# Sums of weights in DRAM that start in attention's first unit, five accumulations ahead of the differences of values

## The chip, the core and the metric

The kernel runs on one core of one Trainium2 chip. Its time is device microseconds of one execution, from the first to the last instruction with what lies around them. A core has five engines with a queue of instructions each: PE (TensorE, matmul), DVE (VectorE), ACT (ScalarE), POOL (GpSimd) and SP (SyncE, which here only starts transfers). An engine takes its instructions in order; one that waits on a semaphore holds up all behind it. SP's transfers and POOL's transfers go through two queues (q1 and q0 in the profile) to the same 16 DMA engines.

## The reference, cut to what matters

One layer: normalization, windowed attention with a gate, a projection, an embedding with a second gate, a last normalization.

```python
hn = rmsnorm(x, norm_g[i])
y = swa_mixer(hn, swa_w_in[j], swa_w_out[j], swa_sinks[j], rel_bias)   # attention over 128 keys, (out * silu(gate)) @ w_out
x = x + y
emb = p[i] @ ple_proj[i]
g = jax.nn.sigmoid(rmsnorm(x, ple_norm[i]) @ ple_gate[i])
x = x + emb * g
return rmsnorm(x, final_g)
```

512 rows, width 2048, 32 heads of 64 over 4 key heads, all in f32. The two products that matter here are `(out * silu(gate)) @ w_out` and `rmsnorm(x) @ ple_gate`, both 512 x 2048 by 2048 x 2048.

## The kernel before, in words

Every f32 product is made of three matmuls on a high and a low part (lines 126 to 128). A weight block of 128 x 1024 comes in over SP's queue (`wraw` while the query and gate projections run, `braw` afterwards), ACT casts its high part (`whi`, `bhi`: lines 109 and 774), DVE subtracts the low part (`wlo`, `blo`: lines 110 and 775), and PE takes both.

The program has three stretches. First 16 steps over the width make keys, values and the first queries. Then comes **attention**, a loop of 64 units (8 pairs of heads x 8 groups of rows, with three more passes that drain it): each unit issues scores, softmax, transposition and values for one group and, between them, a share of the projections that are left, so that PE always has a matmul to do. The order on all five engines is that of the Python code in this loop (a manual schedule). At last come the **output product** with `w_out` and then the product with `ple_gate`, each by a fast scheme with seven products of half-size matrices instead of eight; PE and SP keep the code's order there, too.

The fast scheme needs sums of weight blocks (product 7 takes block (1,2) plus block (2,2), for instance). They are formed in DRAM while attention runs, without an arithmetic engine, in two steps each: SP copies one block to a scratch tensor (`small_w_out`, `w_out`, `ple_gate`; line 732, 0.5 MB each), and POOL issues a transfer that adds the second block to it in DRAM (line 734). `sum_weights(i)` takes step i: even steps are copies, odd ones accumulations, and accumulation n stands at step 2n + 7, so it follows its copy by some steps. There are 64 copies and 64 accumulations in 134 steps. An accumulation waits on POOL until its copy has landed. Eight more blocks, `ple_gate` 6, are copied from the sums of product 7 (`copy_six`, line 720) and accumulated later (`add_six`, line 724): four of them at attention's end and four in the output product.

`sums_in(i)` says which steps stand at the end of unit i. Before: the eight copies of steps 0, 2, ..., 14 in unit 0; the accumulations of the first 16 steps in units 1 to 3; the remaining 118 steps spread over units 4 to 63.

Other work on POOL that the change stands next to: `make_diff` (lines 437 and 438) forms differences of values of neighbouring blocks, which ACT and DVE then split (lines 376 and 377) and SP spreads over the partitions (`DV`, line 446); line 504 puts a softmax tile's sink column in place, which DVE's maximum (line 525) needs; line 575 masks a tile. After attention POOL issues the first load of x for the residual sum, line 1043, which DVE's addition at line 1138 needs. On SP the copies stand among the loads of `wraw` (line 102), of `twice` and `DV` (lines 428, 446), and of biases (line 467).

Of the kernel before, what the change touches and what calls it, by code (L numbers as in the profile page):

```python
# [55 lines left out]
def trunk_kernel(ctx: ExitStack, tc: tile.TileContext, a: dict):  # L56
# [298 lines left out]
    def make_key(h):  # L355

        t, e = divmod(h, 2)
        k = K[h] = kvq.tile([P, S // QB, 2, QB], F32R, tag="k", name=f"k{h}", bufs=2)
        same = slice(64 * e, 64 * e + 64)

        def part(low):
            src = kt[t][same].rearrange("p (j k) -> p j k", k=QB)
            for o in (slice(0, 64), slice(64, 128)):
                if low:
                    nc.vector.tensor_sub(k[o, :, 1], src, k[same, :, 0].bitcast(F32))
                else:
                    nc.scalar.copy(k[o, :, 0], src)

        return partial_of(part, False), partial_of(part, True)
# [4 lines left out]
    def split(dst, v):  # L374
        return (
            lambda: nc.scalar.copy(dst[:, :, 0, :], heads(v)),
            lambda: nc.vector.tensor_sub(dst[:, :, 1, :], heads(v), dst[:, :, 0, :].bitcast(F32)),
        )
# [22 lines left out]
    for b in range(exact, BUCKETS):  # L401
        d = np.nonzero(bk == b)[0]
        if len(d):
            lo, n = P - 1 + int(d.min()), len(d)
# [20 lines left out]
    def spread_first():  # L425
        src = V[0][:HB].rearrange("p h l d -> p (h l d)").bitcast(F32)
        for o in range(2):
            nc.sync.dma_start(twice[HB * o : HB * o + HB].bitcast(F32), src)
    diffs = {}

    def make_diff(n):
        if n == 1:
            diffs["all"] = quarter("diffs").rearrange("p k t -> p (k t)")
        w = KVH * HD
        v = values[0] if n == 3 else diffs["all"][:, 3 * S + (n - 1) * w : 3 * S + n * w]
        lower, upper = slice(0, HB), slice(HB, P)
        nc.gpsimd.tensor_sub(v[lower], values[n][lower], values[n - 1][lower])
        nc.gpsimd.tensor_sub(v[upper], values[n - 1][upper], values[n][upper])
        dst = diffs["all"][:, (n - 1) * S : n * S].bitcast(F32R)
        diffs[n] = split(dst.rearrange("p (h l d) -> p h l d", h=KVH, l=2), v)  # L440

    def spread_diff(n):
        src = diffs["all"][:, (n - 1) * S : n * S]
        for b in range(2):
            for o in range(2):
                nc.sync.dma_start(DV[HB * o : HB * o + HB, n - 1, b].bitcast(F32), src[HB * b : HB * b + HB])

    def first_chores(i, step):

        if step == 0 and i < NB - 1:  # L450
            make_diff(i + 1)
        if step == 0 and i == 1:
            spread_first()
        if step and 1 <= i < NB:
            diffs[i][step - 1]()
        if step == 2 and 1 <= i - 1 < NB:
            spread_diff(i - 1)
        if step and 1 <= i - 2 < NB:
            split(V[i - 2], values[i - 2])[step - 1]()
# [127 lines left out]
    def weigh(i):  # L587

        d, g = divmod(i, UNITS)
        n, b = divmod(g, 2)  # L590
        kv = d // 2
        r, own = PT.pop(i)
        if g == 0:
            U[d] = apool.tile([P, 2, S], F32, tag="u", name=f"u{d}", bufs=3)
        if b == 0:
            O[d] = bank(f"o{i}", "o").rearrange("p (b u e q) -> p b u e q", b=2, u=2, e=2)
        ops = O[d]
        out = ops[:, b].rearrange("p u e q -> p (u e q)")
        first = V[0 if n == 0 else n - 1 + b][:, kv]
        if g == 0:  # L600
            nc.tensor.matmul(out, twice[:, kv * 2 * HD : (kv + 1) * 2 * HD], r[:, 0], start=True, stop=True)
        for low in range(2 if g else 0):
            nc.tensor.matmul(out, first, r[:, low], start=low == 0, stop=own is None and low == 1)  # L603
        if own is not None:
            nc.tensor.matmul(
                out, DV[:, n - 1, b, kv * 2 * HD : (kv + 1) * 2 * HD], own[:, 0], start=False, stop=True
            )
        yield
        if b:
            dst = U[d][:, :, n * P : (n + 1) * P].rearrange("p u (b q) -> p b u q", b=2)  # L610
            lower, upper = slice(0, 64), slice(64, 128)
            tmp = [apool.tile([P, 2, 2, HB], F32, tag=f"tmp{e}", name=f"tmp{e}_{i}", bufs=1) for e in range(2)]
            for e, (o, x) in enumerate(((lower, upper), (upper, lower))):
                nc.scalar.copy(tmp[e][o], ops[x, :, :, e, :])
            for e, o in enumerate((lower, upper)):
                nc.vector.tensor_add(dst[o], ops[o, :, :, e, :], tmp[e][o])
        if g == UNITS - 1:
            for c in (2 * d, 2 * d + 1):
                weighed.add(c)
                if c in open_gates:  # L620
                    idle.append(partial_of(gate_value, c))
# [97 lines left out]
    def copy_six(jj, m):  # L719
        nc.sync.dma_start(summed["ple_gate", 6, jj, m], summed["ple_gate", 7, jj, m])  # L720

    def add_six(jj, m):
        src = block("ple_gate", *MORE[6], jj, m)
        nc.gpsimd.dma_start(summed["ple_gate", 6, jj, m], src, accum_op=ALU.add, max_dma_last_dim=8192)

    SUM_STEPS = 2 * len(copies) + 6
    SUMS_EARLY = 16

    def sum_weights(i):

        if i % 2 == 0 and i // 2 < len(copies):
            nc.sync.dma_start(*copies[i // 2])
        elif i % 2 == 1 and 0 <= i // 2 - 3 < len(adds):
            nc.gpsimd.dma_start(*adds[i // 2 - 3], accum_op=ALU.add, max_dma_last_dim=8192)
# [191 lines left out]
    blocks = TWOS * UNITS  # L926

    def sums_in(i):


        if i == 0:
            return range(0, SUMS_EARLY, 2)
        if i < 4:
            return range(4 * i + 3, min(4 * i + 7, SUMS_EARLY), 2)
        n, of = SUM_STEPS - SUMS_EARLY, blocks - 4
        return range(SUMS_EARLY + (i - 4) * n // of, SUMS_EARLY + (i - 3) * n // of)

    six_copied = {blocks - 3: (0, 1), blocks - 2: (2, 3)}
    six_added = {blocks - 1: (0,), blocks: (1,), blocks + 1: (2,), blocks + 2: (3,)}

    left = KC * (len(kinds) - 1)

    def some(of, n=1):
        for _ in range(min(n, len(of))):
            of.pop(0)()

    softmax = iter(())
    for i in range(blocks + 3):

        before, softmax = softmax, scores(i) if i < blocks else iter(())  # L950
        turned = turn(i - 2) if 2 <= i < blocks + 2 else iter(())
        value = weigh(i - 3) if 3 <= i else iter(())
        next(turned, None)
        next(value, None)
        next(softmax, None)
        next(turned, None)
        next(before, None)
        next(softmax, None)
        first_chores(i, 0)
        if i in (6, 20, 36):  # L960
            idle.extend(make_key(1 + i // 16))
        todo = left // (blocks + 2 - i) if i < blocks + 2 else 0
        left -= todo
        for n in range(max(todo, 6)):
            if n < todo:
                next(proj)
            if n == 0:
                first_chores(i, 1)
                some(W.todo)
                some(chores or idle)  # L970
            elif n == 2:
                next(turned, None)
                next(value, None)
                if len(chores) > 1:
                    some(chores)
            elif n == 3:
                next(softmax, None)
            elif n == 4:
                first_chores(i, 2)
                some(chores or idle)  # L980
            elif n == 5:
                next(softmax, None)
        if i < blocks:
            for n in sums_in(i):
                sum_weights(n)
        for m in six_copied.get(i, ()):
            copy_six(0, m)
        for m in six_added.get(i, ()):
            add_six(0, m)
# [778 lines left out]
    n = done[3]  # L1768
# [81 lines left out]
```

## Time and profile before

| | us |
|---|---|
| median of 3 runs | 782.78 (782.68 to 783.89) |
| the profiled execution's own time | 782.67 |
| span of that execution, first to last instruction | 781.0 |
| PE busy in it | 770.9 |
| DVE, ACT, POOL busy | 618.5, 529.0, 171.1 |
| mean granted TensorE clock | 0.996 |

The span is read first by engine, then by the waits of the engine that is busy all the time. In a row of the timeline stand the start in us, the duration in us, the engine, the line, the operation and its tiles, and in brackets the idle time of the engine just before it with what ended it. [...]

### The profile page before, as it was taken

The numbers are of one execution on the slowest core, as the hardware profiler recorded it, in microseconds if no ns is written. First come the engines' busy times: TensorE is split into PE (matmuls) and PEld (weight loads), VectorE is DVE, ScalarE is ACT, GpSimd is POOL, SyncE is SP. The second block draws the span as 40 slices with busy tenths as digits, with TensorE's granted clock in tenths as the row PEclk, the third lists the DMA queues.
The fourth block names the chain that finished last, engine by engine and source line by source line (L and its number), as shares of the span: only waits on it lengthen the run. The fifth ranks groups of instructions, "written<-read, shape, count | busy, mean of one in ns | idle before, by whom it ended". The sixth has DMA issues, their size and how long they took to land.

```text
span 781.0 us, 11165 instructions
## 1 busy us (share of the span) xinstructions
PE 770.9 (99%) x3652; PEld 643.7 (82%) x3652; DVE 618.5 (79%) x1069; ACT 529.0 (68%) x1121; POOL 171.1 (22%) x311
## 2 busy tenths in 40 slices
PE   9999999999999999999999999999999999999995
PEld 8888888888888888888888877888888888888885
DVE  4555697876877688777877789978799889998996
ACT  6753586766776676766766645577766888867874
POOL 0200523122232313132322300112101121221111
PEclk9999999999999999999999999999999999999998
DMA  9978899999999989999999999999899999899956
GB/s 347 300 210 296 186 276 300 280 295 274 272 255 275 280 232 286 276 277 268 268 276 292 221 309 322 359 311 283 317 390 337 304 301 354 264 263 309 322 140 216
DMA packets 53306, 221.41 MB, mean 284 GB/s; under 512 B 8240, under 2 KB 9264, under 8 KB 46848
## 3 DMA queue, kind: packets, MB, share of 16 engines
q1 hardware_dynamic: 39408, 158.77, 57.1%
q0 software_dynamic: 13840, 61.93, 37.1%
q8 instruction: 29, 0.48, 0.2%
q14 instruction: 29, 0.24, 0.1%
HBM read 203.84 MB, written 87.08 MB: 373 GB/s over the span
## 4 chain that ended last, share of the span: by engine, by line
PE 98%; issue 1%; DVE 0%; POOL 0%; POOLq 0%; DVEq 0%
PE gps L126 7%; PE gps L127 7%; PE gps L128 7%; PE qps L126 7%; PE qps L127 7%; PE qps L128 7%; PE o L127 6%; PE o L128 5%; PE o L126 5%; PE g L126 5%; PE g L128 5%; PE g L127 5%; PE s L485 2%; PE vps L290 2%; PE o L603 2%; PE pt L551 2%
## 5 line engine op out<-in xcount | busy, mean ns | idle before, releaser
L774 ACT CAST bhi<-braw 128x1024 fp32r<-128x1024 f32 x100 | 105.1, 1052 | 52.6 <-PE o L128 15.2
L775 DVE TENSOR_TENSOR blo<-braw,bhi 128x1024 fp32r<-128x1024 f32 x100 | 121.5, 1220 | 22.0 <-ACT bhi L774 21.2
L126 PE MATMUL gps<-xh,whi 128*128 128x512 f32 x256 | 100.0, 390 | 0.0
L127 PE MATMUL gps<-xl,whi 128*128 128x512 f32 x256 | 99.9, 390 | 0.0
L128 PE MATMUL gps<-xh,wlo 128*128 128x512 f32 x256 | 99.8, 390 | 0.0
L126 PE MATMUL qps<-xh,whi 128*128 128x512 f32 x224 | 87.8, 392 | 0.0
L128 PE MATMUL qps<-xh,wlo 128*128 128x512 f32 x224 | 87.5, 390 | 0.0
L127 PE MATMUL qps<-xl,whi 128*128 128x512 f32 x224 | 87.4, 390 | 0.0
L575 POOL TENSOR_SCALAR_AFFINE_SELECT own<-r 64x512 fp32r<-64x512 f32 (+1 forms) x48 | 32.5, 677 | 236.8 <-DVE r L565 236.8
L127 PE MATMUL o<-blo,fho 128*128 128x512 f32 x192 | 75.2, 392 | 0.7 <-DVE blo L775 0.7
L110 DVE TENSOR_TENSOR wlo<-wraw,whi 128x1024 fp32r<-128x1024 f32 x60 | 73.5, 1226 | 2.8 <-ACT whi L109 2.7
L126 PE MATMUL o<-bhi,fho 128*128 128x512 f32 x192 | 74.8, 390 | 0.0
L128 PE MATMUL o<-bhi,flo 128*128 128x512 f32 x192 | 74.7, 389 | 0.0
L109 ACT CAST whi<-wraw 128x1024 fp32r<-128x1024 f32 x60 | 62.3, 1040 | 4.7 <-issue 4.1
L126 PE MATMUL g<-bhi,fhg 128*128 128x512 f32 x160 | 62.3, 390 | 0.0
L127 PE MATMUL g<-blo,fhg 128*128 128x512 f32 x160 | 62.3, 389 | 0.0
L128 PE MATMUL g<-bhi,flg 128*128 128x512 f32 x160 | 62.2, 389 | 0.0
L128 PEld LDWEIGHTS gps<-xh,wlo 128*128 128x128 f32 x256 | 48.1, 188 | 10.3
L126 PEld LDWEIGHTS gps<-xh,whi 128*128 128x128 f32 x256 | 48.1, 188 | 9.1
L529 ACT ACTIVATE t<-t,sm 128x129 f32<-128x129 f32 (+1 forms) x128 | 49.6, 389 | 8.7 <-DVE sm L525 7.4
L127 PEld LDWEIGHTS gps<-xl,whi 128*128 128x128 f32 x256 | 48.1, 188 | 8.9
L564 ACT CAST r<-pt 128x256 fp32r<-128x256 f32 x56 | 20.9, 372 | 49.8 <-PE pt L551 49.3
(299 smaller groups left out, 1831.8 us busy)
## 6 DMA issues: line engine op xcount, KB each, us to landing
wraw<-in_w_gate_in SPq DMA_DIRECT2D x32, 512.0 KB, 7.5
w_out<-in_w_out POOLq DMA_DIRECT2D x32, 512.0 KB, 8.9
braw<-w_out SPq DMA_DIRECT2D x32, 512.0 KB, 7.8
wraw<-in_w_q SPq DMA_DIRECT2D x28, 512.0 KB, 7.0
ple_gate<-in_ple_gate POOLq DMA_DIRECT2D x24, 512.0 KB, 9.2
braw<-in_w_out SPq DMA_DIRECT2D x22, 512.0 KB, 7.5
braw<-in_ple_gate SPq DMA_DIRECT2D x22, 512.0 KB, 6.7
xw<-in_first SPq DMA_DIRECT2D x14, 640.5 KB, 6.7
```

The lines of the kernel that those rows point to most:

```text
L109: nc.scalar.copy(hi, raw)
L110: nc.vector.tensor_sub(lo, raw, hi.bitcast(F32))
L126: nc.tensor.matmul(ps, sh, mh, start=first, stop=False, skip_group_check=more)
L127: nc.tensor.matmul(ps, sh, ml, start=False, stop=False, skip_group_check=more)
L128: nc.tensor.matmul(ps, sl, mh, start=False, stop=last, skip_group_check=more)
L290: nc.tensor.matmul(v_ps[t], h[:, c], part_of(high_at, 256, 512), start=f, stop=e, skip_group_check=True)
L485: nc.tensor.matmul(s_ps[:, u, : 2 * n], st, of_keys[:, first * 2 * QB : (first * QB + n) * 2], start=True, stop=True)
L529: nc.scalar.activation(su, su, AF.Exp, bias=sm[:, u : u + 1], accum_out=sm[:, 2 + u : 3 + u])
L564: nc.scalar.copy(rh, src)
L575: nc.gpsimd.affine_select(out=flat(own), in_=flat(r).bitcast(F32), pattern=[[0, 8], [sign, HB]], compare_op=ALU.is_ge, fill=0.0, base=-HB ...
L774: nc.scalar.copy(hi[:, :n], raw)
L775: nc.vector.tensor_sub(lo[:, :n], raw, hi[:, :n].bitcast(F32))
```

## The change

The eight copies of the first steps and five accumulations (steps 7, 9, 11, 13 and 15) now stand together in unit 0, behind the unit's scores and ahead of `first_chores(0, 0)`, which calls `make_diff(1)`. Unit 0 has no sums at its end. The remaining 118 steps are spread over units 1 to 60 instead of 4 to 63. The four extra copies stand one per unit in units 59 to 62 (before: two each in units 61 and 62), and their accumulations in units 61 to 64 (before: 63 to 66). What is copied and added, and the number of transfers, is the same.

```diff
-    SUMS_EARLY = 16
+    SUMS_EARLY, FIRST_SUMS = 16, 1
...
     def sums_in(i):
-        if i == 0:
-            return range(0, SUMS_EARLY, 2)
-        if i < 4:
-            return range(4 * i + 3, min(4 * i + 7, SUMS_EARLY), 2)
+        if i < FIRST_SUMS:
+            return ()
         n, of = SUM_STEPS - SUMS_EARLY, blocks - 4
-        return range(SUMS_EARLY + (i - 4) * n // of, SUMS_EARLY + (i - 3) * n // of)
-
-    six_copied = {blocks - 3: (0, 1), blocks - 2: (2, 3)}
-    six_added = {blocks - 1: (0,), blocks: (1,), blocks + 1: (2,), blocks + 2: (3,)}
+        i -= FIRST_SUMS
+        return range(SUMS_EARLY + i * n // of, min(SUMS_EARLY + (i + 1) * n // of, SUM_STEPS))
+
+    six_copied = {blocks - 5: (0,), blocks - 4: (1,), blocks - 3: (2,), blocks - 2: (3,)}
+    six_added = {blocks - 3: (0,), blocks - 2: (1,), blocks - 1: (2,), blocks: (3,)}
...
         next(softmax, None)
+        if i == 0:
+            for n in (*range(0, SUMS_EARLY, 2), *range(7, SUMS_EARLY, 2)):
+                sum_weights(n)
         first_chores(i, 0)
```

Three places show what that does to the queues. **POOL, units 0 to 2** (from line 504's first tile on; `t` is the softmax tile of a unit). Before:

```order
L504 COPY t_908<-sinkb 128x2
L507 MEMSET t_908 128x32
L437 TENSOR_TENSOR diffs<-values 64x256
L438 TENSOR_TENSOR diffs<-values 64x256
L504 COPY t_965<-sinkb 128x2
L507 MEMSET t_965 128x32
L437 TENSOR_TENSOR diffs<-values 64x256
L438 TENSOR_TENSOR diffs<-values 64x256
L734 DMA small_w_out_0_772<-in_w_out 64x2048
L734 DMA small_w_out_1_773<-in_w_out 64x2048
```

And now:

```order
L504 COPY t_908<-sinkb 128x2
L507 MEMSET t_908 128x32
L734 DMA small_w_out_0_772<-in_w_out 64x2048
L734 DMA small_w_out_1_773<-in_w_out 64x2048
L734 DMA w_out_0_0_774<-in_w_out 64x2048
L734 DMA w_out_0_1_775<-in_w_out 64x2048
L734 DMA w_out_0_2_776<-in_w_out 64x2048
L437 TENSOR_TENSOR diffs<-values 64x256
L438 TENSOR_TENSOR diffs<-values 64x256
L504 COPY t_970<-sinkb 128x2
L507 MEMSET t_970 128x32
```

The five accumulations, each of which waits for its copy, stand ahead of the first difference and of the next unit's sink column.

**SP, units 0 to 2**, as a piece of the difference: `wraw_924` before and `wraw_937` now is the same weight block.

```order
 L102 DMA wraw_886<-in_w_q 128x1024
-L102 DMA wraw_924<-in_w_q 128x1024
 L732 DMA small_w_out_0_772<-in_w_out 16x8192
 L732 DMA small_w_out_1_773<-in_w_out 16x8192
...
 L732 DMA w_out_1_1_779<-in_w_out 16x8192
+L102 DMA wraw_937<-in_w_q 128x1024
 L428 DMA twice<-V_716 64x512 x2
-L102 DMA wraw_1036<-in_w_gate_in 128x1024
+L732 DMA w_out_1_2_780<-in_w_out 16x8192
+L102 DMA wraw_1040<-in_w_gate_in 128x1024
 L446 DMA DV<-diffs 64x512 x4
-L102 DMA wraw_1102<-in_w_gate_in 128x1024
+L732 DMA w_out_1_3_781<-in_w_out 16x8192
+L102 DMA wraw_1106<-in_w_gate_in 128x1024
```

One weight block goes from ahead of the eight copies to behind them, and the next three copies (`w_out_1_2`, `w_out_1_3` and one more) each stand ahead of a weight block that had no copy ahead of it.

**POOL at attention's end** (`ple_gate` 6, with line 724; `x1s` is the residual sum). Before:

```order
L734 DMA small_ple_gate_1_835<-in_ple_gate 64x2048
L724 DMA ple_gate_0_0_836<-in_ple_gate 64x2048
L575 AFFINE_SELECT own_4929<-r_4923 64x512
L724 DMA ple_gate_0_1_837<-in_ple_gate 64x2048
L575 AFFINE_SELECT own_5004<-r_4997 128x512
L724 DMA ple_gate_0_2_838<-in_ple_gate 64x2048
L724 DMA ple_gate_0_3_839<-in_ple_gate 64x2048
L1043 DMA x1s<-in_x 128x4x512
```

And now (the load of x has line 1045):

```order
L724 DMA ple_gate_0_1_837<-in_ple_gate 64x2048
L504 COPY t_4879<-sinkb 128x2
L575 AFFINE_SELECT own_4881<-r_4869 128x512
L724 DMA ple_gate_0_2_838<-in_ple_gate 64x2048
L575 AFFINE_SELECT own_4931<-r_4925 64x512
L724 DMA ple_gate_0_3_839<-in_ple_gate 64x2048
L575 AFFINE_SELECT own_5006<-r_4999 128x512
L1045 DMA x1s<-in_x 128x4x512
```

Before, two accumulations stood right ahead of the load of x; now the last one is ahead of a mask, and none stands between that mask and the load.

## The prediction

> **What bounds the kernel now.** I read the page first by engine, then by its chain.
>
> ```profile
> PE 770.9 (99%) x3652; PEld 643.7 (82%) x3652; DVE 618.5 (79%) x1069; ACT 529.0 (68%) x1121; POOL 171.1 (22%) x311
> ...
> PE 98%; issue 1%; DVE 0%; POOL 0%; POOLq 0%; DVEq 0%
> ```
>
> PE is busy for 770.9 of 781.0 us, and it is 98% of the chain that ended last. So the change, which touches neither PE's instructions nor their number, can win only where PE waits, and lose only where it makes PE wait. The waits of PE, by whom it waited for, have one row besides the program's start:
>
> ```profile
> PE o L127 <- DVE blo L775: 0.7, 1, 0.7
> ```
>
> The chain in order of time shows where these 0.7 us come from:
>
> ```profile
> 464.73 0.53 DVE x1s L1138
> 465.33 1.22 DVE gate L878
> 466.55 1.14 DVE blo L775
> ...
> 766.01 6.42 issue
> ```
>
> At 464 us, early in the output product, the chain leaves PE for three DVE instructions, of which the first is the addition to the residual sum. The 6.42 us at 766 belong to the end of the program, which the change does not reach. So the ceiling of a gain is at 464 us, and the risk is in attention.
>
> **The change at attention's end: what it may win.** Line 1138 waits for the sums of one PE bank and for the load of x that POOL issues (line 1043). On POOL, and by the view of the transfers (KB each, us to landing):
>
> ```profile
> 433.52 0.66 POOL L575 TENSOR_SCALAR_AFFINE_SELECT own<-r 128x512 fp32r<-128x512 f32 x1 [4.06 <-DVE r L565]
> ...
> 447.99 1.61 POOL L724 DMA_DIRECT2D ple_gate<-in_ple_gate  x2
> 450.41 0.83 POOL L1043 DMA_DIRECT2D x1s<-in_x  x1 [0.81 <-PE o L603]
> ```
>
> ```profile
> x1s<-in_x SPq DMA_DIRECT2D x3, 1024.0 KB, 8.1
> ...
> x1s<-in_x POOLq DMA_DIRECT2D x1, 1024.0 KB, 13.6
> ```
>
> The load is issued at 450.41 and lands 13.6 us later, at 464.0; three loads of the same size on SP's queue need 8.1 us (median). Right ahead of it in POOL's queue are two accumulations of 447.99. What DVE and PE did around the landing:
>
> ```profile
> 462.24 1.23 DVE L775 TENSOR_TENSOR blo<-braw,bhi 128x1024 fp32r<-128x1024 f32 x1 [1.75 <-ACT bhi L774]
> 464.12 1.28 DVE L1138 TENSOR_TENSOR x1s<-x1s,o 128x512 f32<-128x512 f32 x2 [0.66 <-PE o L128]
> ...
> 466.47 1.22 DVE L775 TENSOR_TENSOR blo<-braw,bhi 128x1024 fp32r<-128x1024 f32 x1
> ```
>
> ```profile
> 464.13 1.05 ACT L774 CAST bhi<-braw 128x1024 fp32r<-128x1024 f32 x1 [1.93 <-PE o L128]
> ```
>
> ```profile
> 450.30 0.40 PE L126 MATMUL o<-bhi,fho 128*128 128x512 f32 x1
> ...
> 465.97 0.39 PE L126 MATMUL o<-bhi,fho 128*128 128x512 f32 x1
> ...
> 466.65 0.39 PE L126 MATMUL o<-bhi,fho 128*128 128x512 f32 x1
> 467.74 0.50 PE L127 MATMUL o<-blo,fho 128*128 128x512 f32 x1 [0.70 <-DVE blo L775]
> ...
> 470.61 0.50 PE L127 MATMUL o<-blo,fho 128*128 128x512 f32 x1
> ...
> 476.69 0.40 PE L128 MATMUL o<-bhi,flo 128*128 128x512 f32 x1
> ```
>
> DVE sat idle for 0.66 us until 464.12. The row names a matmul, but the two banks that are added were complete after the first 48 matmuls of the product (2 halves of the rows x 8 pieces of the width x 3), which begins at 450.30: at about 461.2, some 3 us before. The landing at 464.0 fits. PE then started a matmul at 467.74, 1.09 us after the one ahead of it instead of the usual 0.227 (three starts from 465.97 to 466.65 are 0.68 us): 0.86 us lost. Three more pauses of 0.11 us follow (one behind each DVE subtraction, like that at 470.61), as DVE has no room from there on. In all, the 38 starts from 466.65 to 476.69 take 10.04 us where 38 x 0.2268 = 8.62 would do: 1.42 us too much.
>
> With the change the last accumulation is issued a unit ahead of the load instead of 1 us ahead. By the SP loads x then lands at 450.41 + 8.1 = 458.5, before line 775 has even begun at 462.24. The addition can start at 462.24 + 1.23 = 463.47, so everything behind it is 0.65 us earlier: that is the near bound of the gain. The far bound is the whole 1.42: if the weight block ahead also lands sooner (DVE's 1.75 us of idle time before 462.24), the subtraction at 466.47 is held only by ACT's cast, which ends at 464.13 + 1.05 = 465.18, 1.29 us before, and that is more than the 0.86. The zero bound holds if something else releases line 1138 at the same moment. I take **-1.0 us**, midway between 0.65 and 1.42, since the near term is certain if the load is the cause and DVE's idle time ahead of it is of the same kind.
>
> The price there: each of the four extra accumulations waits on POOL for its copy, two units before it, and behind it stand the sink column and the mask of the next unit. Two units are 2 x 5.7 us, and the eight copies of line 720 landed in 6.8 to 11.7 us:
>
> ```profile
> DMA to landing us min/median/max: 6.8/9.2/11.7
> ```
>
> At worst POOL waits 0.3 us there, against 4.06 us of idle time ahead of each mask (433.52). Cost: 0; without that cover 0.3 us.
>
> **The change at attention's start: what it may lose.** Nothing is computed more; POOL is blocked from the first accumulation on, and one weight block queues behind eight copies. Ahead of the change:
>
> ```profile
> 77.09 0.73 POOL L437 TENSOR_TENSOR diffs<-values 64x256 f32<-64x256 f32 x1 [18.55 <-DVE values L388]
> ...
> 81.38 1.69 POOL L734 DMA_DIRECT2D small_w_out<-in_w_out  x2
> ```
>
> ```profile
> L732 SPq DMA_DIRECT2D w_out<-in_w_out x1: 587/587/587, 63.1 to 63.1; - x1
> ...
> DMA to landing us min/median/max: 11.5/11.5/11.5
> ```
>
> POOL idles 18.55 us before the first difference, to 77.09. The fifth copy, issued at 63.1, landed at 74.6, so with copies as fast as before the fifth accumulation (0.8 us to issue, half of 1.69) is out by 75.4, and the differences lose nothing. That is the near end. But the accumulations now run beside the copies. How long one keeps the DMA engines is seen between 85 and 95 us, where POOL's queue has them almost alone (packets, MB, share):
>
> ```profile
> q0 software_dynamic: 295, 1.97, 98.6%
> ```
>
> 0.524 MB at 0.197 MB a us are 2.7 us. If all four earlier accumulations go ahead of the fifth copy, it lands at 74.6 + 10.7 = 85.3; the fifth is issued by 86.1, the first difference (two pieces of 0.73 and their gaps, 1.6 us) is there at 87.7 and the sink column at 87.9. That is the far end. Who waits:
>
> ```profile
> 86.69 0.39 ACT L376 CAST diffs<-diffs 128x256 fp32r<-128x256 f32 x1
> 88.35 0.41 ACT L529 ACTIVATE t<-t,sm 128x129 f32<-128x129 f32 x1 [1.27 <-DVE sm L525]
> ```
>
> ```profile
> 87.90 0.42 DVE L525 TENSOR_REDUCE sm<-t 128x2 f32<-128x258 f32 x1
> ```
>
> ACT would lose 1.0 us at 86.69 and get it back from the 1.27 us that it idles before 88.35; DVE's maximum at 87.90 has its column just in time. Cost at either end: 0. If ACT's cover were gone, 1.0 us.
>
> The weight block behind the copies is needed by ACT's cast at 93.68. The fifth of the eight copies landed at 74.6, and between 75 and 80 us the DMA engines ran dry (0.12 below), so the copies were done by about 78. A block of 0.524 MB at the 324 GB/s of the row for 70 to 75 us takes 1.6 us: it lands at about 80 at the near end and, behind five accumulations, at 80 + 13.5 = 93.5 at the far one, where ACT just has it. Cost: 0.
>
> ```profile
> 93.68 1.04 ACT L109 CAST whi<-wraw 128x1024 fp32r<-128x1024 f32 x1
> ```
>
> What is left is the sum of the traffic. Three more copies (1.6 us each) and two more accumulations come before 105 us: 4.8 + 5.4 = 10.2 us of DMA time. Free time before was, by stretches of 5 us (the DMA engines' share stands in the column before the last, GB/s in the last):
>
> ```profile
> 70.00:75.00 5.00, 5.00 (x24) 4.12 (x23) 4.17 (x7) 1.91 (x4) 0.00 (x0) 1.00 1.00 324
> 75.00:80.00 5.00, 5.00 (x24) 4.14 (x23) 4.86 (x11) 1.36 (x2) 2.69 (x6) 1.00 0.12 46
> 80.00:85.00 5.00, 5.00 (x25) 4.17 (x24) 3.44 (x8) 2.67 (x3) 4.88 (x6) 1.00 0.86 188
> ...
> 100.00:105.00 5.00, 5.00 (x26) 4.24 (x25) 4.79 (x10) 2.69 (x10) 0.59 (x1) 1.00 0.72 160
> ```
>
> 4.4 + 0.7 + 1.4 = 6.5 us, so the transfers fall behind by up to 3.7 us once. The block loaded at 103.53 in 4.9 us (108.4) is cast at 110.11, 1.7 us later; the probabilities that ACT wrote just ahead of that cast, by 109.92, are transposed by PE at 113.45, another 3.5 us. 3.7 is less than 5.2: cost 0, with 1.5 us to spare.
>
> ```profile
> 103.53 0.53 SPq L102 DMA_DIRECT2D wraw<-in_w_q  x1
> ```
>
> ```profile
> 109.22 0.70 ACT L542 ACTIVATE pr<-t,sm 128x128 f32<-128x128 f32 x2 [0.65 <-DVE sm L531]
> ...
> 110.11 1.04 ACT L109 CAST whi<-wraw 128x1024 fp32r<-128x1024 f32 x1
> ```
>
> ```profile
> 113.45 0.38 PE L551 MATMUL pt<-ident,pr 128*128 128x128 f32 x2
> ```
>
> [...]
>
> **The sum.** 782.67 (the profiled execution's own time) - 1.0 (output product) + 0 (start) + 0 (end of attention) = 781.67. The median of the runs lies 0.11 above that execution, so the forecast is **781.8 us**.
>
> **Rivals.** *A, the forecast*: -0.4 to -1.4, chance 0.55. *B, the wait is only renamed*: the addition starts sooner, but DVE still reaches the same subtraction late, or line 1138 was in truth held by PE, as its row says. For it: that row, and the ACT row that is released at the same moment. Against: the bank is complete 3 us before. Time: 782.7, chance 0.25. *C, the transfers fall behind at the start*: the moved work takes more than the 10.2 us that I count, because copies and accumulations that run together slow each other. It decides from (6.5 + 5.2) / 10.2 = 1.15 times on; at 1.4 times it is 14.3 - 6.5 - 5.2 = 2.6 us of PE waiting at the transpositions between 95 and 120 us. For it: the DMA shares of 1.0 in most slices of the page. Against: PE never waited in attention at the same shares. Time: 781.8 + 2.6 = 784.4 with the gain kept, 785.4 without; chance 0.13. *D, more than the whole pause*: the 1.42 us go and the ordinary spread of runs helps: 781.2 or less, chance 0.07.
>
> **How the numbers follow.** A measurement of this kernel tells about 0.2%, 1.57 us, from no change: 781.2 to 784.35 counts as the same. Faster: D and the edge of A, 0.11. Slower: C at 1.4 times and above, 0.09; its milder forms count as the same. Same: 0.80. Range: A reaches from 781.2 to 782.4 by its bounds; with B and the milder half of C it is **781.0 to 783.8**.
>
> **What would show it.** *Right*: PE's start at 467.74 closes up, line 1138 has no idle time before it, the load of x lands in some 8 us; the five accumulations stand between 67 and 86 us on POOL, each held by a copy; PE has no wait in attention. *Wrong*: a wait of PE on a transposition or on ACT between 85 and 120 us, an ACT cast there that waits for `wraw` for over 3 us, or line 1138 still idle to 464.

## The result, and the profile after

| | before | changed |
|---|---|---|
| median (range) of 6 runs, us | 783.06 (782.36 to 783.89) | 787.51 (787.14 to 788.42) |
| profiled execution's own time, us | 782.67 | 787.76 |
| span, us | 781.0 | 786.0 |

The ratio is 1.0057, with an interval of 1.0044 to 1.0070: the change makes the kernel 0.57% slower. 787.5 lies above the whole predicted range (781.0 to 783.8). Two of the ten executions of one kernel below (e12), the profiled one among them, took 1583 and 2016 us; its ratio leaves them out, and its waits aren't listed.

The page of the changed kernel, by engine and then by its chain, and the waits of PE by whom it waited for:

```profile
PE 772.8 (98%) x3652; PEld 646.1 (82%) x3652; DVE 618.7 (79%) x1069; ACT 528.9 (67%) x1121; POOL 168.0 (21%) x311
...
PE 91%; DMA 5%; DVE 2%; issue 1%; ACT 0%; POOL 0%; POOLq 0%; SPq 0%; DVEq 0%
```

```profile
PE o L605 <- ACT own L585: 3.8, 2, 3.4
```

The wait for line 775 in the output product is gone. A new one has come: PE waits 3.8 us for ACT, and DMA, which had no share in the chain, holds 5% of it. One matmul per unit (line 605, probabilities times values) shows when the time was lost. Before, by the timeline of PE:

```profile
108.25 0.28 PE L605 MATMUL o<-own,DV 128*128 128x256 f32 x1
...
113.92 0.28 PE L605 MATMUL o<-own,DV 128*128 128x256 f32 x1
...
119.59 0.28 PE L605 MATMUL o<-own,DV 128*128 128x256 f32 x1
...
125.27 0.28 PE L605 MATMUL o<-own,DV 128*128 128x256 f32 x1
```

The same four in the changed kernel, with what PE did behind the second wait:

```profile
108.90 0.28 PE L605 MATMUL o<-own,DV 128*128 128x256 f32 x1
...
115.15 0.39 PE L605 MATMUL o<-own,DV 128*128 128x256 f32 x1 [0.42 <-ACT own L585]
...
124.50 0.39 PE L605 MATMUL o<-own,DV 128*128 128x256 f32 x1 [3.42 <-ACT own L585]
...
125.75 0.63 PE L126 MATMUL qps<-xh,whi 128*128 128x512 f32 x1
126.17 0.63 PE L127 MATMUL qps<-xl,whi 128*128 128x512 f32 x1
...
131.89 0.28 PE L605 MATMUL o<-own,DV 128*128 128x256 f32 x1
```

The distance to before is 0.65, 1.23, 4.91 and 6.62 us. The first 0.65 are there ahead of any wait and are the ordinary difference of two executions (the first load of `twice` leaves SP at 79.23 us before, at 79.88 here, and between 79.19 and 80.13 in the other kernels below). The two waits add 0.58 and 3.68; the first, small one is not followed further here. The last 1.71 us come without a wait: matmuls of 512 columns start 0.42 us apart (125.75 to 126.17) instead of 0.227, because the granted clock fell. By the table of stretches, with the clock in the column PEclk, third from the end:

```profile
124.00:126.00 2.00, 1.50 (x7) 1.33 (x8) 0.74 (x3) 1.92 (x8) 0.00 (x0) 0.91 1.05 307
126.00:128.00 2.00, 2.00 (x6) 1.54 (x6) 1.91 (x5) 0.64 (x4) 0.00 (x0) 0.50 0.92 375
128.00:130.00 2.00, 2.00 (x8) 1.62 (x7) 1.90 (x6) 1.77 (x4) 1.66 (x4) 0.74 1.00 410
```

At half speed for all of the middle stretch, and for 0.36 and 1.04 us of the others (four times what each mean lacks to 1), that is 3.40 us, which cost 1.70.

From there the distance stays until the output product. The load of x on POOL is issued at 457.04 (before 450.41: 6.63 later), and DVE's addition now follows its predecessor without idle time:

```profile
467.03 1.22 DVE L775 TENSOR_TENSOR blo<-braw,bhi 128x1024 fp32r<-128x1024 f32 x1
468.16 1.28 DVE L1140 TENSOR_TENSOR x1s<-x1s,o 128x512 f32<-128x512 f32 x2
```

The distance at the program's end is 5.09 us (782.67 to 787.76), so the output product gave back 6.63 - 5.09 = 1.54 us. The account: 0.65 ordinary, 4.26 of waits with what lies around them, 1.71 of clock, less 1.5 in the output product.

**Where the wait comes from.** The chain of the changed kernel in order of time:

```profile
80.44 13.94 DMA twice<-V
94.39 12.43 DMA wraw<-in_w_gate_in
106.84 1.46 DMA bias<-tdram
...
111.78 9.90 DMA wraw<-in_w_q
121.70 1.04 ACT whi L109
122.77 0.62 ACT k L367
123.40 0.61 ACT k L367
124.04 0.41 ACT own L585
...
124.50 0.39 PE o L605
```

Read from the end: PE wants `own`, which ACT casts behind two casts of keys and behind the cast of a weight block; the block was issued at 111.78 and took 9.90 us. Before, the same block (the fourth weight block behind `twice` on SP) was issued and cast here:

```profile
107.62 0.53 SPq L102 DMA_DIRECT2D wraw<-in_w_q  x1
```

```profile
114.99 1.04 ACT L109 CAST whi<-wraw 128x1024 fp32r<-128x1024 f32 x1
...
117.33 0.41 ACT L585 CAST own<-own 64x256 fp32r<-64x256 f32 x1
```

It landed in 6.1 us, at 113.7. That left 1.3 us to ACT's cast, and `own`, done at 117.74, left another 1.85 us to PE's 119.59: 3.1 us of cover. In the changed kernel the block lands at 121.68, or 121.0 without the ordinary 0.65: 7.3 us later. 7.3 - 3.1 = 4.2 us, which is where PE stands behind the second wait (4.26). Half of the 7.3 (3.5 us) is the later issue on SP, half (3.8 us) the slower landing (9.9 for 6.1).

SP is late because it, too, waited. Its queue in the changed kernel:

```profile
81.76 0.53 SPq L102 DMA_DIRECT2D wraw<-in_w_gate_in  x1
...
91.80 0.60 SPq L732 DMA_DIRECT2D w_out<-in_w_out  x1
94.39 0.34 SPq L102 DMA_DIRECT2D wraw<-in_w_gate_in  x1
97.65 5.82 SPq L446 DMA_DIRECT2D DV<-diffs  x4
103.52 0.60 SPq L732 DMA_DIRECT2D small_w_out<-in_w_out  x1
```

What SP waited for, and the time to landing of the weight block of 81.76:

```profile
SPq L446 <- DMA wraw<-in_w_gate_in: 3.6, 1, 3.6
...
SPq L102 <- DMA twice<-V: 2.0, 1, 2.0
```

```profile
DMA to landing us min/median/max: 20.0/20.0/20.0
```

Two transfers that land late hold SP. The weight block at 94.39 waits 2.0 us and leaves in the moment in which the second `twice` lands (80.44 + 13.94); `twice` took 2.3 us before. The second piece of `DV` waits 3.6 us and leaves at 101.7, when the weight block of 81.76 lands; that block took 4.5 us before. In both cases the transfer waited for stands eight places ahead in SP's queue. The first hold does little to the block that matters, as the first piece of `DV` leaves at 97.65, where it left at 97.00 before: the ordinary 0.65. The second one does nearly all: the four pieces of `DV` take 5.82 us of SP instead of 3.14, 2.7 of the 3.5 us. The copy at 103.52, which wasn't there before, adds 0.64, the biases behind it 0.2.

### The profile page after: what moved, and what is told of

It reads as the page before. It is cut to its first block, busy times and chain, and to the rows that moved or that the text cites. A ratio compares the mean times of both kernels' runs of the same rounds, so it can differ in the third digit from the quotient of the medians.

```text
span 786.0 us, 11163 instructions
## 1 busy us (share of the span) xinstructions
PE 772.8 (98%) x3652; PEld 646.1 (82%) x3652; DVE 618.7 (79%) x1069; ACT 528.9 (67%) x1121; POOL 168.0 (21%) x311
## 4 chain that ended last, share of the span: by engine, by line
PE 91%; DMA 5%; DVE 2%; issue 1%; ACT 0%; POOL 0%; POOLq 0%; SPq 0%; DVEq 0%
PE gps L126 7%; PE gps L127 7%; PE gps L128 6%; PE qps L126 6%; PE qps L127 6%; PE qps L128 6%; PE o L127 6%; PE o L126 6%; PE o L128 6%; PE g L128 5%; PE g L127 5%; PE g L126 5%; PE s L485 2%; DMA twice<-V 2%; PE vps L290 2%; PE o L603 2%
## 5 line engine op out<-in xcount | busy, mean ns | idle before, releaser
L575 POOL TENSOR_SCALAR_AFFINE_SELECT own<-r 64x512 fp32r<-64x512 f32 (+1 forms) x48 | 32.4, 675 | 244.2 <-DVE r L565 231.0
L565 DVE TENSOR_TENSOR r<-pt,r 128x256 fp32r<-128x256 f32 x56 | 23.7, 424 | 38.9 <-ACT r L564 38.1
```

The source lines that it names most:

```text
L565: nc.vector.tensor_sub(rl, src, rh.bitcast(F32))
L575: nc.gpsimd.affine_select(out=flat(own), in_=flat(r).bitcast(F32), pattern=[[0, 8], [sign, HB]], compare_op=ALU.is_ge, fill=0.0, base=-HB ...
```

## The experiments

All are made from the two kernels by a few lines; where nothing is said, a run computes everything. Times are medians, compared with the kernel before on the same chip (783.28, 782.98 and 783.36 us in the three batches); the ratio is taken over the single executions and need not be the quotient of two medians. "Five" are the accumulations ahead of the differences of values, "rest" the 118 steps behind the first 16, "tail" the four extra copies and accumulations at attention's end. The last column is what POOL's queue moved between 80 and 120 us, and the share of the DMA engines' time that it took.

| kernel | five | rest in units | tail | us | ratio | PE's wait for `own`, us | POOL's queue |
|---|---|---|---|---|---|---|---|
| before | no | 4 to 63 | before | 783.06 | | 0 | 3.28 MB, 41.8% |
| changed | yes | 1 to 60 | changed | 787.51 | 1.0057 [1.0044, 1.0070] | 3.8 | 4.07 MB, 50.1% |
| e2 | no | 1 to 60 | changed | 789.12 | 1.0075 [1.0060, 1.0090] | 5.3 | 4.65 MB, 58.0% |
| e9 | yes | 3 to 62 | before | 784.09 | 1.0013 [1.0000, 1.0027] | 1.7 | 2.97 MB, 37.6% |
| e3 | no | 4 to 60 | changed | 787.69 | 1.0049 [1.0026, 1.0072] | 6.2 | 3.69 MB, 49.7% |
| e1 | yes | 4 to 60 | changed | 782.28 | 0.9998 [0.9982, 1.0013] | 1.5 | 3.07 MB, 39.2% |
| e12 | no | 6 to 60 | changed | 781.62 | 0.9978 [0.9969, 0.9988] | | |
| e6 | yes | 6 to 60 | changed | 781.36 | 0.9980 [0.9971, 0.9990] | 0 | 2.47 MB, 32.4% |
| e5 | no | 4 to 63 | changed | 781.52 | 0.9983 [0.9973, 0.9992] | 0 | 3.20 MB, 40.8% |
| e10 | yes | 4 to 63 | changed | 781.36 | 0.9975 [0.9965, 0.9986] | 0 | 2.33 MB, 28.5% |

### The five alone (e1)

Against the changed kernel, the rest begins in unit 4 again and still ends with unit 60:

```diff
-        if i < FIRST_SUMS:
+        if i < 4:
             return ()
-        n, of = SUM_STEPS - SUMS_EARLY, blocks - 4
-        i -= FIRST_SUMS
+        n, of = SUM_STEPS - SUMS_EARLY, blocks - 7
+        i -= 4
```

> The changed kernel, but units 1 to 3 hold no sums: the remaining 118 steps are spread over units 4 to 60 instead of 1 to 60. The eight copies and five accumulations stay in unit 0. Theory 1 (PE's 3.8 us of waiting come from the transfers that moved into units 1 to 3, on top of the five): no wait of PE near 124 us, the output product's gain stays, about 781.5 us. Theory 2 (the five accumulations ahead of the differences are enough: the load of the first values takes 13.9 us behind them and holds SP): the wait stays, about 787 us, and that load still takes some 14 us.

Measured: 782.28 us, in single runs from 781.17 to 787.41. Most of the loss is gone, so the five alone don't make it. A wait of PE of 1.5 us is left, at the same place:

```profile
118.45 1.05 ACT L109 CAST whi<-wraw 128x1024 fp32r<-128x1024 f32 x1 [3.32 <-DMA wraw<-in_w_q]
```

It is the same weight block that ACT waits for. The runs scatter over 6 us, as they would where the block lands close to the end of its cover.

### The early rest alone (e2)

Against the changed kernel: the first 16 steps as before (so the lines that the change put into unit 0 are out), the rest over units 1 to 60.

```diff
+        if i == 0:
+            return range(0, SUMS_EARLY, 2)
+        early = range(4 * i + 3, min(4 * i + 7, SUMS_EARLY), 2) if i < 4 else ()
...
+        rest = range(SUMS_EARLY + (i - 1) * n // of, min(SUMS_EARLY + i * n // of, SUM_STEPS))
+        return (*early, *rest)
```

> The kernel before with its start (copies at the end of unit 0, five accumulations in units 1 to 3), but the remaining 118 steps begin in unit 1 as in the changed kernel, and its end of attention. Theory 1 (traffic of units 1 to 3): the same wait or a longer one, since all accumulations now fall in units 1 to 3: 787 us or more. Theory 2 (the five ahead): no wait, about 781.5 us.

Measured: 789.12 us, more than the whole change. `twice` lands in 2.3 us here, as before, and PE still waits 5.3 us. The queues of this kernel between 80 and 120 us (packets, MB, share):

```profile
q0 software_dynamic: 696, 4.65, 58.0%
```

Against 3.28 MB and 41.8% before, that is 1.37 MB more of accumulations in the stretch in which the weight blocks of units 4 to 6 are loaded. The two waits (3.29 and 2.05 us) fall on earlier blocks: the first goes back to the block issued at 91.81, which takes 18.4 us to land. So the early rest is sufficient, and the five, which take accumulations out of this stretch, even make it milder (4.07 MB in the changed kernel).

### Neither, but the shorter spread (e3)

Against the changed kernel: units 0 to 3 as before (again without the lines in unit 0), the rest over units 4 to 60. That is 2.07 steps per unit instead of 1.97.

```diff
+        if i == 0:
+            return range(0, SUMS_EARLY, 2)
+        if i < 4:
+            return range(4 * i + 3, min(4 * i + 7, SUMS_EARLY), 2)
+        n, of = SUM_STEPS - SUMS_EARLY, blocks - 7
+        return range(SUMS_EARLY + (i - 4) * n // of, min(SUMS_EARLY + (i - 3) * n // of, SUM_STEPS))
```

> The kernel before in units 0 to 3; the remaining steps over units 4 to 60, and attention's end as in the changed kernel (four extra copies in units 59 to 62, accumulations in 61 to 64). Both theories: no wait at the start, and only the output product's gain of 1.0 to 1.5 us: 781.3 to 781.8 us. If the gain in the output product were an effect of the late start, it would be missing: 782.8 us.

Measured: 787.69 us, from 783.49 to 790.72. No wait was expected at all. The profiled execution (790.72 us) shows one wait of 6.2 us at 126.43, again for `own` behind the cast of that block, and a longer dip of the clock (0.50 in the stretch left out, too):

```profile
124.00:126.00 2.00, 0.00 (x0) 0.00 (x0) 1.23 (x1) 1.94 (x4) 0.00 (x0) 0.82 1.05 436
126.00:128.00 2.00, 1.57 (x5) 1.48 (x6) 0.81 (x2) 1.94 (x8) 0.00 (x0) 0.50 0.59 182
...
130.00:132.00 2.00, 2.00 (x6) 1.55 (x5) 1.90 (x6) 1.71 (x4) 1.66 (x4) 0.50 0.92 369
132.00:134.00 2.00, 2.00 (x10) 1.61 (x9) 1.46 (x2) 0.50 (x1) 0.00 (x0) 0.97 0.80 152
```

Steps that only come a little denser from unit 4 on are enough. So the kernel before stood just inside its cover, and what counts is how much is queued beside the blocks of units 4 to 6, not the change's units 1 to 3 as such. e1 has the same spread with the five in unit 0 and loses far less (782.28), so with this spread the five are better early.

### Without the five accumulations (e4)

The changed kernel with the five left out: their sums are not formed, only copied.

```diff
-            for n in (*range(0, SUMS_EARLY, 2), *range(7, SUMS_EARLY, 2)):
+            for n in range(0, SUMS_EARLY, 2):
                 sum_weights(n)
```

> The changed kernel with the five accumulations of unit 0 left out (five sums of weights lack their second block). Both theories take 5 x 2.7 = 13.5 us of DMA time away between 67 and 95 us: no wait of PE near 124 us, about 781.5 us, and the load of the first values lands in 2 to 4 us. If the wait stays, the accumulations are not its cause, but the order on SP (eight copies ahead of a weight block, one more copy per unit) is: about 787 us.

Measured in one execution: 781.29 us, no wait of PE for `own`, `twice` in 2.3 us, 2.18 MB on POOL's queue between 80 and 120. With 2.6 MB less to move, the early rest costs nothing, though SP's order is that of the changed kernel. This looks as if the five were to blame, but it only takes away load: in the first experiment they are there, and most of the loss is not.

### The tail alone (e5)

The kernel before with only the four extra copies and accumulations moved:

```diff
-    six_copied = {blocks - 3: (0, 1), blocks - 2: (2, 3)}
-    six_added = {blocks - 1: (0,), blocks: (1,), blocks + 1: (2,), blocks + 2: (3,)}
+    six_copied = {blocks - 5: (0,), blocks - 4: (1,), blocks - 3: (2,), blocks - 2: (3,)}
+    six_added = {blocks - 3: (0,), blocks - 2: (1,), blocks - 1: (2,), blocks: (3,)}
```

> The kernel before, with nothing changed but the four extra copies (units 59 to 62) and their accumulations (61 to 64); the 118 steps stay in units 4 to 63. Theory: the waits of PE between 105 and 130 us depend on how many accumulations stand ahead of the weight blocks there, which is as before here, so none; the output product's gain is left: 781.3 to 781.8 us, faster than before by 1 to 1.5 us. Rival: the gain needs the other accumulations to end sooner, too: 782.8 us.

Measured: 781.52 us, ratio 0.9983 [0.9973, 0.9992], 1.46 us less than before in the same batch. In DVE's timeline the subtraction ahead of the addition has come forward with it:

```profile
460.88 1.22 DVE L775 TENSOR_TENSOR blo<-braw,bhi 128x1024 fp32r<-128x1024 f32 x1
462.02 1.27 DVE L1138 TENSOR_TENSOR x1s<-x1s,o 128x512 f32<-128x512 f32 x2
```

Before, line 775 began at 462.24 behind 1.75 us of idle time and the addition at 464.12. The whole pause is gone, as it is in the changed kernel.

### The five, and a gap behind them (e6)

The changed kernel with the rest over units 6 to 60, so that units 1 to 5 have no sums:

```diff
-        if i < FIRST_SUMS:
+        if i < 6:
             return ()
-        n, of = SUM_STEPS - SUMS_EARLY, blocks - 4
-        i -= FIRST_SUMS
+        n, of = SUM_STEPS - SUMS_EARLY, blocks - 9
+        i -= 6
```

> The changed kernel, with no sums in units 1 to 5: the remaining 118 steps over units 6 to 60. Theory: the five accumulations fill the DMA engines' idle stretch from 75 to 80 us, no accumulation and no copy stands beside the weight blocks loaded at 102 to 113 us, so PE doesn't wait: 781.3 us in all runs, as without the five accumulations (781.29). Rival (the five themselves make the later blocks late): a wait near 121 us in some runs, as with the steps from unit 4 on, 782 to 787 us.

Measured: 781.36 us, no wait, although `twice` still takes 13.1 and 15.1 us. So a late `twice`, by itself, is covered.

### One accumulation earlier (e7)

The kernel before with the sixth accumulation (step 17) in unit 4 instead of unit 5:

```diff
-        return range(SUMS_EARLY + (i - 4) * n // of, SUMS_EARLY + (i - 3) * n // of)
+        steps = [*range(SUMS_EARLY + (i - 4) * n // of, SUMS_EARLY + (i - 3) * n // of)]
+        return [s for s in steps if s != 17] + [17] * (i == 4)
```

> The kernel before, with one accumulation (the sixth, step 17) in unit 4 instead of unit 5, nothing else. Theory: this one accumulation of some 2.7 us, issued at about 105 us, goes ahead of the copies and weight blocks of 106 to 110 us and makes the block that ACT casts at 115 us late: a wait of PE on ACT near 121 us of 1 to 6 us in some runs, 783 to 790 us. Rival (the waits come from the denser sums, 2.07 steps per unit, or the copies): as before, 783.3 us.

Measured: 783.55 us, ratio 1.0006 [0.9996, 1.0015], no wait for `own`, against the theory. One accumulation a unit sooner is not enough to use up the cover.

### Three of the five (e8)

The changed kernel with the last two of the five left out:

```diff
-            for n in (*range(0, SUMS_EARLY, 2), *range(7, SUMS_EARLY, 2)):
+            for n in (*range(0, SUMS_EARLY, 2), *range(7, SUMS_EARLY - 4, 2)):
```

> The changed kernel with the last two of the five accumulations of unit 0 left out (two sums lack their second block). How the load of the first values (two transfers, issued at 79.9 us) fares behind accumulations in flight: if it has to wait until they have drained, it lands 5.4 us sooner than behind five, in 8 us; if the two queues took turns by small packets, it would be served within about 3 us behind three as behind five, and its 13.9 us would have another cause. PE's wait near 124 us: shorter than 3.8 us or none, 781.3 to 784 us.

Measured in one execution: 785.59 us, PE waits 3.3 us for `own`, and `twice` takes 13.6 and 15.8 us, as with five. If `twice` waited for the accumulations ahead of it to drain, each would have its share in the delay. In these single executions that theory falls: three delay it as much as five do, and none (e4) not at all. The 3 us of the other case, an estimate of the author's, didn't come either.

### The early rest in milder form (e9)

The changed kernel with the rest over units 3 to 62 and the tail of before:

```diff
-    SUMS_EARLY, FIRST_SUMS = 16, 1
+    SUMS_EARLY, FIRST_SUMS = 16, 3
...
+    six_copied = {blocks - 3: (0, 1), blocks - 2: (2, 3)}
+    six_added = {blocks - 1: (0,), blocks: (1,), blocks + 1: (2,), blocks + 2: (3,)}
```

> The changed kernel with the remaining steps over units 3 to 62 instead of 1 to 60 (and attention's end as before, so without the output product's gain of 1.5 us). How the wait grows with the shift: one unit earlier than before. Theory (each unit earlier adds about one copy and one accumulation, some 4 us of transfers, ahead of the weight block that was 1.3 us early): a wait of 0 to 2 us near 121 us, 783 to 785 us. Rival (only the shift by three units is too much): as before, 783.0 us.

Measured: 784.09 us, from 782.38 to 787.30, ratio 1.0013 [1.0000, 1.0027]. PE waits 1.7 us for `own` and 1.0 in the output product:

```profile
122.31 0.38 PE L605 MATMUL o<-own,DV 128*128 128x256 f32 x1 [1.66 <-ACT own L585]
```

The wait is milder than from unit 1, and it is there although POOL's queue moves less than before between 80 and 120 us (2.97 against 3.28 MB). The volume alone doesn't decide it, then.

### The five, with the rest where it was (e10)

The changed kernel with the rest over units 4 to 63 again:

```diff
-    SUMS_EARLY, FIRST_SUMS = 16, 1
+    SUMS_EARLY, FIRST_SUMS = 16, 4
```

> The changed kernel with the remaining 118 steps back over units 4 to 63, as before the change; the eight copies and five accumulations in unit 0 and attention's end stay. Theory (the lost time comes from the transfers moved into units 1 to 3, not from the five): no wait of PE at 105 to 130 us, 781.4 us, like the kernel in which only attention's end is changed (781.52). Rival (the five are part of it): a wait near 121 us, 783 us or more.

Measured: 781.36 us, from 781.05 to 782.01, ratio 0.9975 [0.9965, 0.9986]: faster than both kernels, with one number changed. The queue of POOL between 80 and 120 us, and SP's `DV` that took 5.82 us in the changed kernel:

```profile
q0 software_dynamic: 364, 2.33, 28.5%
```

```profile
96.97 2.67 SPq L446 DMA_DIRECT2D DV<-diffs  x4
```

With the rest back in its place the five cost nothing; taking back the early rest takes away the whole loss. Whether they add something to the tail's gain (781.52 without, 781.36 with them) can't be told.

### Without the next two accumulations (e11)

The changed kernel with steps 17 and 19 left out: the two accumulations that the early rest moves to the front most, while its copies stay where they are.

```diff
-                sum_weights(n)
+                if n not in (17, 19):
+                    sum_weights(n)
```

> The changed kernel with the sixth and seventh accumulations (steps 17 and 19, on POOL at 84 and 88 us) left out; SP's order is the same. Theory 1 (volume of transfers): 5.4 us of transfers less ahead of the weight blocks, so PE's 3.8 us of waiting go, 781.5 us. Theory 2 (SP's order: one copy more ahead of each weight block, and the wait for the transfer eight places before): the wait stays above 2 us, 784 us or more.

Measured in one execution: 783.62 us, PE's wait is 1.7 us instead of 3.8, and the clock doesn't fall (2.93 MB are left on POOL's queue). SP's part of the delay is gone, with SP's order unchanged: the weight block behind `twice` lands in 15.6 us instead of 20.0, no piece of `DV` has to wait for it, and the decisive block leaves SP at 107.29 (before: 107.62). What is left is its slower landing, 11.8 us instead of 6.1. So the order on SP costs nothing by itself here; it passes on what a late landing ahead costs.

### The gap without the five (e12)

The kernel before with the rest over units 6 to 60 and the changed tail (its lines are those of e5):

```diff
-        n, of = SUM_STEPS - SUMS_EARLY, blocks - 4
+        n, of = SUM_STEPS - SUMS_EARLY, blocks - 9
+        i -= 6
...
```

> The kernel before in units 0 to 3 (five accumulations in units 1 to 3), no sums in units 4 and 5, the remaining steps over units 6 to 60, attention's end as changed. Beside the kernel with the five in unit 0 and the same gap (781.36): if the five ahead of the differences are worth anything by themselves, this one is slower than 781.4, with a wait at 121 us in some runs; if they are neutral, it is 781.4 as well.

Measured: 781.62 us, ratio 0.9978 [0.9969, 0.9988], against 0.9980 [0.9971, 0.9990] with the five (e6). Where the following units leave room, their place makes no difference.

### The decisive block in each kernel

Before, ACT cast this block at 114.99, and PE could have waited another 1.85 us: a landing past 116.84 must show as a wait. Here are the profiled executions, with the ordinary difference (by the first `twice`, 79.23 before) taken off the times of issue and landing:

| kernel | issued by SP | us to landing | landing behind 116.84, us | PE's wait for `own`, us |
|---|---|---|---|---|
| before | 107.62 | 6.1 | -3.1 | 0 |
| e10 | 106.66 | 6.0 | -4.2 | 0 |
| e7 | 107.63 | 7.7 | -1.5 | 0 |
| e4 | 106.72 | 9.7 | -0.4 | 0 |
| e1 | 106.66 | 11.7 | 1.5 | 1.5 |
| e9 | 106.69 | 11.9 | 1.7 | 1.7 |
| e11 | 106.83 | 11.8 | 1.8 | 1.7 |
| e8 | 109.90 | 10.6 | 3.7 | 3.3, in two |
| changed | 111.13 | 9.9 | 4.2 | 3.8, in two |
| e3 | 107.91 | 15.2 | 6.3 | 6.2 |

The cover gives every wait. In e1, e3, e9 and e11 SP is on time and the slower landing makes all of it. Each kernel here that waits has an accumulation in unit 4 and another in unit 5 (on POOL at 107.48 and 112.61 in the changed kernel, at 105.95 and 111.09 in e9); so has e4, which escapes by 0.4 us. Before, the first of them comes at 110.39, 3.3 us ahead of the block's landing. The one in unit 4 alone (e7) makes the block 1.6 us slower.

## Why the prediction was wrong

**What bounds the kernel: right.** Gain and loss lie where the prediction placed them: the gain at the addition to the residual sum, the risk in attention between 85 and 120 us.

**The output product: right, at the far bound.** The prediction took 1.0 us, midway between 0.65 and 1.42. It measured 1.5 in the profile and 1.46 by the tail alone. The load of x lands in 5.6 us, where some 8 were forecast (13.6 before). The far bound's condition holds: the weight block ahead also comes sooner (line 775 at 460.88), so DVE's 1.75 us go too.

**POOL and the five accumulations: right.** Their cost was put at 0, with a near end of 75.4 and a far end of 86.1 for the fifth. By POOL's timeline of the changed kernel it came at the near end, and the first difference waited for DVE, not for POOL:

```profile
67.40 0.87 POOL L734 DMA_DIRECT2D small_w_out<-in_w_out  x1 [7.14 <-DMA small_w_out<-in_w_out]
...
74.75 0.77 POOL L734 DMA_DIRECT2D w_out<-in_w_out  x1 [1.21 <-DMA w_out<-in_w_out]
77.75 0.73 POOL L437 TENSOR_TENSOR diffs<-values 64x256 f32<-64x256 f32 x1 [2.23 <-DVE values L388]
```

77.75 is 77.09 and the ordinary 0.65. The fifth copy landed at 74.5, as before (74.6), with accumulations issued beside it from 67.40 on; the last three copies came later than before (the eighth at 82.8 instead of 77.7).

**The weight block behind the copies: right.** It landed at 88.8, inside 80 to 93.5, ahead of its cast.

**The step that failed: "3.7 is less than 5.2: cost 0".** Both numbers were wrong.
- The *cover* was that of the block issued at 103.53. The next need for data was taken to be the transposition behind it. The probabilities stand ahead of this block's cast on ACT (109.22 against 110.11), so a late cast doesn't hold them; behind it stands `own`, done at 112.67, which PE takes at 113.92. So the cover was 1.7 + 1.25, some 3.0 us, not 5.2. And three blocks leave SP between 103.5 and 108.8, each with its own cast; the one issued at 107.62 had 1.3 us to its cast and 1.85 us more to PE, 3.1 in all. The scarcest cover of the stretch sets the cost, and no other block was considered. Even the 3.7 us of the prediction would have cost 0.6 there. ACT's row behind the cast of 110.11, before:

```profile
112.26 0.41 ACT L585 CAST own<-own 64x256 fp32r<-64x256 f32 x1
```

- The *delay* was 7.3 us, not 3.7. The sum asked only how much more the DMA engines had to move. About half of the delay, 3.5 us, is SP's: its transfers went out in the code's order, a piece of `DV` had to wait for the weight block eight places ahead, which took 20.0 us, and the prediction took SP's queue only for what stands ahead of what. The other half is the block's own landing, 9.9 us instead of 6.1.
- A wait had no *price beyond its length* in the prediction. Behind the 3.4 us one, the clock added 1.7.

Rival C named this mechanism, copies and accumulations that slow each other, and the point from which it decides (1.15 times). Its price of 2.6 us was less than half of what came (4.26 + 1.71), and a chance of 0.13 was too little for a forecast that had 1.5 us to spare on a sum of 10. Its argument against, that PE never waited at the same DMA shares, says nothing about how near to waiting it was: in e3, 5% more steps per unit, which brings an accumulation into unit 4, suffice.

The prediction's own signs were there: a wait of PE on ACT, and an ACT cast held by `wraw` for over 3 us (4.18):

```profile
121.70 1.04 ACT L109 CAST whi<-wraw 128x1024 fp32r<-128x1024 f32 x1 [4.18 <-DMA wraw<-in_w_q]
```

**What stays open** is how the slower landing divides between the accumulations and the copies beside the block: with an accumulation in each of units 4 and 5 it takes 9.7 us in e4, 11.8 in e11 and 15.2 in e3. e4, e8 and e11 are single executions. A kernel with the weight blocks on a queue of their own would tell more; it wasn't tried.

## What to carry to other kernels

When transfers are moved to the front of a phase that is bound by compute, go through every load of that phase, not one: landing, first use, and from there to the matmul; the smallest of these sums is the cover, and the price begins where the delay passes it. Ask also which later issues the same queue must hold until a delayed transfer lands (here SP held a piece of `DV` for 3.6 us). A change with two halves (here a sooner start for a sooner end) deserves a version with each half alone: the sooner end won 1.5 us by itself and needed nothing of the sooner start.

## What the runs showed of the hardware

**A stall of PE cost more than its length in three kernels.** Of the seven kernels whose profiled execution waits for `own`, three show a dip of the granted clock to 0.50. It lasts 3.40 us in the changed kernel, where it cost 1.70, and 6.84 us in e3 (by the rows above: 0.72 + 6 + 0.12). In e2 two waits stand close together, and the dip follows the second, shorter one (2.05 us, ending at 119.68), not the first (3.29 us, ending at 111.71):

```profile
110.00:112.00 2.00, 0.29 (x2) 0.29 (x3) 0.73 (x1) 1.76 (x3) 0.00 (x0) 1.00 0.92 196
...
120.00:122.00 2.00, 2.00 (x8) 1.61 (x7) 1.92 (x5) 1.55 (x7) 0.14 (x1) 0.58 0.92 349
122.00:124.00 2.00, 2.00 (x6) 1.57 (x6) 1.32 (x4) 0.06 (x1) 1.46 (x3) 0.56 1.27 422
```

It lasts 1.68 + 1.76 = 3.44 us. Waits of 2.07 (e8), 1.71 (e11), 1.66 (e9) and 1.47 us (e1) had no dip. So the length of a wait didn't decide it by itself: one of 2.05 us was followed by a dip, those of 2.07 and 3.29 us were not.

Nor does the dip begin at a fixed distance from the wait's end. By the rows, it begins at 125.64 in the changed kernel, 1.14 us behind the end of the wait (124.50), at 120.32 in e2, 0.64 us behind it, and at 125.28 in e3, 1.15 us before the wait ends (126.43). In the 3.40 us right ahead of it PE was idle for 2.26, 2.05 and 3.40 us. What makes the clock fall behind one wait and not behind another, and why e3's dip lasts twice as long as the others, these traces don't show.

**While both queues had work, packets went nearly one for one here, and bytes did not.** Between 83 and 91 us of the changed kernel POOL's queue holds accumulations, and SP's holds the weight block of 67.18, `twice`, a copy and the weight block of 81.76 (packets, MB, share):

```profile
q0 software_dynamic: 214, 1.40, 85.2%
q1 hardware_dynamic: 211, 0.53, 19.3%
```

With 214 packets to 211 the accumulations move 2.6 times the bytes and take 85.2% of the engines' time. In e8 it is 205 packets to 220 between 83.0 and 91.1 us. What stands on SP's queue then is slow: in the changed kernel `twice` takes 11.6 and 13.9 us instead of 2.3, the weight block of 81.76 takes 20.0 instead of 4.5. That fits e8, too: with three of the five, accumulations still land until 96.7 us (the one issued at 88.2 takes 8.5), so POOL's queue isn't empty before `twice` is through (96.2).
